# Row factors in place of the padding, the neighbourhood bias from 157 numbers per partition, and the first normalised block scaled on VectorE

## The chip, the cores and the metric

The kernel runs on one core of a Trainium2 chip. A core has five engines that run their own instruction queues side by side and meet at semaphores: TensorE (PE, matrix products), VectorE (DVE) and ScalarE (ACT, both element by element), GpSimd (POOL, a general engine) and SyncE (SP, which here issues every transfer between memory and the core). Data lie in an on-chip memory of 128 partitions; a tile is a rectangle of partitions by bytes in each. The metric is the device time of one execution in microseconds (us), less is better.

## What is computed

Two different transformer blocks follow one another on 256 tokens of width 1024, two layers each, in float32. Shortened to what matters here:

```
x = layer_norm(x, ln_in_g, ln_in_b)
for l in range(2):                                   # first block
    proj = x @ w_in[l]                               # 6816 columns: three attentions and gates
    na   = neighbourhood_attention(...)              # scores + rpb bias, masked, softmax
    df   = diff_attention(...)
    mla  = latent_attention(...)
    merged = sum(gate_i * (branch_i @ w_branch[l, i]))
    x = layer_norm(ALPHA * x + merged @ w_out[l])
    gu = x @ w_ffn_in[l]
    x = layer_norm(ALPHA * x + (silu(gu[:2816]) * gu[2816:]) @ w_ffn_out[l])
for i in range(2):                                   # second block
    ... norm, projection w_in_2, attention and spatial gating, w_o_2
    ... norm, w_up_2, depthwise convolution, silu * up, w_down_2

# neighbourhood attention, head h: tokens on a 4 x 64 grid
sc = q @ k.T * 64 ** -0.5
sc = sc + rpb[h, row offset, column offset]          # rpb: (8 heads, 15, 31)
sc = where(column inside the query's own 16, sc, -inf)
```

## The kernel before

Every large product is made of float32r matmuls on numbers split in two: a high part `hi` and a rest `lo`. `mm3` adds hi x hi, hi x lo and lo x hi into one accumulator, so lines L254, L255 and L256 are its three matmuls. The activations of a stage lie in the tiles `xh` and `xl` (8 chunks of 128 rows by 256 tokens). The weights come by SyncE in blocks called `raw` (up to 1 MB, three buffers, L183). ACT casts a piece of a block into its high part (`high`, L188), DVE subtracts it for the low part (`low`, L192), both into slots of the pool `s4` (30 slots of 4608 bytes). When a block's last piece is split, `low` issues the next block's transfer. A matmul has a stationary operand (128 columns that are loaded first) and a moving operand (256 or 512 columns). `gemm_a` holds the activations stationary and moves 512 columns of weights (a row of the profile names it `ps<-s,xh`: out, moving, stationary). `gemm_b` holds the weights stationary and moves the 256 tokens (`ps<-xh,s`); there the splits are stored 64 bytes (high) and 192 bytes (low) into their slot (`OFF_HI`, `OFF_LO`). Where the activations are themselves in `s4`, as for a branch's output or the FFN's inner values, the rows read `ps<-s,s`.

The order is the program's own: a list of steps that `emit` walks through, in which `turns` mixes attention heads with products (`fill`), and `pump` splits the next pieces ahead of use. Nothing is reordered when it runs: each engine takes its queue in order.

Neighbourhood attention (in each of the first block's two layers) runs eight heads. `na_bias(h)` loads the bias of a head for the 128 query partitions: a partition is a query's (reversed) column in one of two grid rows, and takes 64 numbers of each of four grid rows from `rpb`, at an address that grows by one number from partition to partition. The mask (0 or -1e30) is then added on GpSimd (L852). `na_scores(h)` first calls `na_bias(h + 3)`, then makes the scores, adds the bias on DVE (L863) and takes the softmax; ACT scales the result (L829) and TensorE transposes it (L406). The tiles for these come from the pool `s2`, 12 buffers of 2048 bytes.

At the start `head` normalises the tokens by halves (`t`): statistics on DVE (L493), transposes on TensorE (L530), scale and shift by `ln_in` on ACT (`in_high`, L537, four activations), a cast into `xh` (L538), and the rest into `xl` on DVE (`in_low`, L542).

The tiles that live for the whole program are allocated in `constants`, one behind the other, each rounded up to 32 bytes; behind them lie the pools `raw`, `s4`, `s2`, `gb`, `st`.

Of the kernel before, what the change touches and what calls it, by code (L numbers as in the profile page):

```python
# [10 lines left out]
F32 = mybir.dt.float32  # L11
F32R = mybir.dt.float32r
AF = mybir.ActivationFunctionType
ALU = mybir.AluOpType
# [3 lines left out]
P = 128  # L18
# [8 lines left out]
RMS_EPS = 1e-6  # L27
MASKED = -1e30

X_PAD = 8
WARM = (0, 0)

RAW_BUFS = 3
S4_BUFS = 30
# [79 lines left out]
class Net:  # L116
# [295 lines left out]
    def constants(self):  # L412
        nc, a, cp = self.nc, self.a, self.cp
        self.x_tok = cp.tile([P, 2, D], F32, name="x_tok")
        self.xh = cp.tile([P, KT, 256], F32R, name="xh")
        self.xl = cp.tile([P, KT, 256], F32R, name="xl")
        self.fixed = cp.tile([P, a["c_fixed"].shape[1]], F32, name="fixed")
        cp.tile([P, X_PAD], F32, name="pad")
        self.neghalf = cp.tile([P, 20], F32, name="neghalf")
        nc.vector.memset(self.neghalf, -0.5)  # L420
        self.ones = cp.tile([P, 1], F32, name="ones")
        nc.vector.memset(self.ones, 1.0)
        self.col = cp.tile([P, a["c_vectors"].shape[1]], F32, name="col")
        self.row = cp.tile([P, 2], F32, name="row")
        self.neglam = cp.tile([P, DEPTH], F32, name="neglam")
        for c in range(2):
            cs = slice(c * 512, c * 512 + 512)
            nc.sync.dma_start(self.x_tok[:, 0, cs], a["x"][0, :P, cs])
        nc.sync.dma_start(self.fixed[:, :P + 2 * KT], a["c_fixed"][:, :P + 2 * KT])
        self.ident = self.fixed[:, :P]  # L430
        self.ln_in = [self.fixed[:, P + i * KT:P + (i + 1) * KT] for i in range(2)]
        o = P + 2 * KT

        def table(n):
            nonlocal o
            o += 4 * n
            return self.fixed[:, o - 4 * n:o].rearrange("p (a t n) -> p a t n", a=2, t=2)

        self.rope_df, self.rope_mla, self.rope_gqa = table(16), table(32), table(64)
        self.mask = self.fixed[:, o:o + 64]  # L440
# [91 lines left out]
    def in_high(self, t, c):  # L532
        nc, y, ps = self.nc, self.s2([P, 4, P]), self.in_ps[t, c]
        self.in_y[t, c] = y
        for k in range(4):
            g, b = (v[:, 4 * c + k:4 * c + k + 1] for v in self.ln_in)
            nc.scalar.activation(y[:, k, :], ps[:, k * P:k * P + P], AF.Identity, scale=g, bias=b)  # L537
        nc.scalar.copy(self.xh[:, 4 * c:4 * c + 4, t * P:t * P + P], y)  # L538

    def in_low(self, t, c):  # L540
        ks, ts = slice(4 * c, 4 * c + 4), slice(t * P, t * P + P)
        self.nc.vector.tensor_tensor(self.xl[:, ks, ts], self.in_y[t, c], self.xh[:, ks, ts], op=ALU.subtract)  # L542

    def warm(self, n):

        for _ in range(n):
            self.nc.tensor.matmul(self.warm_ps[:, :P], self.warm_in, self.warm_in, start=True, stop=True)

    def head(self, dfq, dfk):


        self.in_scale, self.in_ps, self.in_y = {}, {}, {}

        def first():
            if WARM[0]:
                self.warm_in, self.warm_ps = self.s2([P, P]), self.psum()
                self.nc.gpsimd.memset(self.warm_in, 1.0)
            self.warm(WARM[0])
            self.in_stats(0)
            self.in_norm(0)  # L560
            self.in_trans(0)
            self.warm(WARM[1])
            self.high(0)
            self.in_high(0, 0)
            self.in_stats(1)
            self.low_next()
            self.in_low(0, 0)
            self.high(1)
            self.low_next()
            self.in_high(0, 1)  # L570
            self.in_norm(1)
            self.in_low(0, 1)

        def second():
            self.in_trans(1)
            self.high(2)
            self.low_next()
            self.high(3)

        def third():  # L580
            self.in_high(1, 0)
            self.low_next()
            self.in_low(1, 0)
            self.in_high(1, 1)

        self.add(first, dfq[:2], second, dfq[2], third, dfq[3], lambda: self.in_low(1, 1), self.lookahead(AHEAD_EDGE), dfq[4:], dfk)

    def in_rows(self, t):
# [62 lines left out]
    def attention_1(self, l):  # L651
        nc, a = self.nc, self.a
        w = a["w_in"][l]
# [187 lines left out]
            S["mlap", h] = (p, sm)  # L841

        def na_bias(h):
            b = self.s2([P, 2, 256])
            rpb = a["na_rpb"]
            for q in range(2):
                for r in range(2):
                    o = rpb.offset + (l * 8 + h) * 465 + (7 - 2 * q - r) * 31 - 48
                    nc.sync.dma_start(b[r * 64:r * 64 + 64, q, :].rearrange("p (r c) -> p r c", r=4),
                                        bass.AP(tensor=rpb.tensor, offset=o, ap=[[1, 64], [31, 4], [1, 64]]))  # L850
            v = b.rearrange("p q (r c) -> p (q r) c", r=4)
            nc.gpsimd.tensor_tensor(v, v, self.mask.unsqueeze(1).broadcast_to([P, 8, 64]), op=ALU.add)  # L852
            S["bias", h] = b

        def na_scores(h):
            if h + 3 < 8:
                na_bias(h + 3)
            ps, p = self.psum("at"), self.s2([P, 512])
            nmx, sm = self.st(2), self.st(2)
            r = slice(64 * (h % 2), 64 * (h % 2) + 64)  # L860
            for q in range(2):
                nc.tensor.matmul(ps[:, q * 256:q * 256 + 256], S["naqT"][r, h // 2, q * P:q * P + P], S["nakT"][r, h // 2, :], start=True, stop=True)
            nc.vector.tensor_tensor(p, ps, S["bias", h].rearrange("p q k -> p (q k)"), op=ALU.add)  # L863
            self.row_exp(p, p, nmx, sm)
            S["nap", h] = (p, sm)
# [88 lines left out]

        fill = gate("df", 1, 0) + late + gate("df", 1, 1) + branch("df", 1, 0, 0) + branch("df", 1, 1, 0) + gate("mla", 2, 0)
        fill.append(Step(lambda: [na_bias(h) for h in range(3)]))
        self.add(turns([(value("mla", "mv"), 3), (trans("mla"), 2), (normalize("mla"), 1), (mla_scores, 0), 1], 8, fill))

# [467 lines left out]
```

## Time and profile before

| | |
|---|---|
| median of 3 runs | 1506.68 us (1506.45 to 1506.7) |
| profiled execution | 1504.22 us, of which the span from first to last instruction is 1502.4 us |
| busy in the span | PE 98%, DVE 66%, ACT 55%, POOL 6% |
| transfers | 260.44 MB, mean 173 GB/s |

The profile is one execution, taken by the hardware. TensorE's matmuls overlap each other in it and their ends are modelled, so how fast it streams is read from the starts of successive matmuls, and how much it loses from its waits. Waits of an engine that is not late for anyone cost nothing.

### The profile page before, as it was taken

To read this page: it belongs to the slowest core of one execution; us is meant where nothing else is said; L and a number is where in the kernel's file an instruction comes from. 1 tells how busy PE (TensorE), PEld (TensorE's weight loads), DVE (VectorE), ACT (ScalarE), POOL (GpSimd) and SP (SyncE) were. 2 spreads that over 40 slices of the span, in tenths; PEclk is the share of its full clock that TensorE was granted. 3 is DMA by queue.
4 is the path that set the end of the run, shared out by engine and by line. 5 is a ranking of instruction groups with operands and counts; after the bars stand their busy time and mean duration, and the time that the engine had idled before them with its cause. 6 is when DMAs were issued, how large, how long until landed. Compare 5 with 4: busy or idle time off the path is not lost.

```text
span 1502.4 us, 23794 instructions
## 1 busy us (share of the span) xinstructions
PE 1478.0 (98%) x9616; PEld 1314.7 (88%) x9616; DVE 990.2 (66%) x1434; ACT 822.8 (55%) x1387; POOL 90.3 (6%) x116
## 2 busy tenths in 40 slices
PE   7999999999999999999999999999999999999998
PEld 5889988899988889998889998777999887789987
DVE  5786655855556676556775555876788758669881
ACT  6664566444442565656444443675767536568660
POOL 0000020000000000011000000310000012000000
PEclk9999999999999999999999999999999999999999
DMA  7744565576563654466665564553565735255660
GB/s 242 249 138 153 177 115 177 168 225 196 193 229 98 203 162 141 147 146 169 201 224 182 178 215 140 183 180 113 164 199 194 254 124 193 74 168 169 199 222 28
DMA packets 179021, 260.44 MB, mean 173 GB/s; under 512 B 23648, under 2 KB 122208, under 8 KB 178912
## 3 DMA queue, kind: packets, MB, share of 16 engines
q1 hardware_dynamic: 178912, 258.93, 54.4%
q8 instruction: 75, 1.23, 0.3%
q14 instruction: 34, 0.28, 0.1%
HBM read 257.86 MB, written 1.05 MB: 172 GB/s over the span
## 4 chain that ended last, share of the span: by engine, by line
PE 48%; DVE 3%; ACT 0%; issue 0%; POOL 0%; DVEq 0%; POOLq 0%; ACTq 0%
PE ps L254 15%; PE ps L256 15%; PE ps L255 15%; DVE s L192 1%; PE ps L1142 1%; PE ps L390 1%; PE ps L406 1%; PE ps L642 0%; DVE x_tok L505 0%; DVE st L493 0%; PE ps L1191 0%; DVE s L492 0%; PE ps L1298 0%; PE ps L1181 0%; DVE s L913 0%
## 5 line engine op out<-in xcount | busy, mean ns | idle before, releaser
L192 DVE TENSOR_TENSOR s<-raw,s 128x1024 fp32r<-128x1024 f32 (+2 forms) x468 | 553.9, 1211 | 175.4 <-ACT s L188 126.6
L188 ACT CAST s<-raw 128x1024 fp32r<-128x1024 f32 (+2 forms) x468 | 466.3, 1039 | 117.1 <-PE ps L255 26.4
L254 PE MATMUL ps<-xh,s 128*128 128x256 f32 x1664 | 475.6, 286 | 1.9 <-DVE s L738 1.4
L255 PE MATMUL ps<-xl,s 128*128 128x256 f32 x1664 | 468.0, 281 | 0.0
L256 PE MATMUL ps<-xh,s 128*128 128x256 f32 x1664 | 466.4, 280 | 0.0
L254 PEld LDWEIGHTS ps<-xh,s 128*128 128x128 f32 x1664 | 313.2, 188 | 10.1 <-issue 6.5
L255 PEld LDWEIGHTS ps<-xl,s 128*128 128x128 f32 x1664 | 317.7, 191 | 0.5
L256 PEld LDWEIGHTS ps<-xh,s 128*128 128x128 f32 x1664 | 314.0, 189 | 0.0
L254 PE MATMUL ps<-s,s 128*128 128x512 f32 (+1 forms) x712 | 259.4, 364 | 0.0
L255 PE MATMUL ps<-s,s 128*128 128x512 f32 (+1 forms) x712 | 254.6, 358 | 0.0
L256 PE MATMUL ps<-s,s 128*128 128x512 f32 (+1 forms) x712 | 254.4, 357 | 0.0
L254 PE MATMUL ps<-s,xh 128*128 128x512 f32 (+3 forms) x448 | 171.8, 383 | 3.6 <-ACT xh L538 3.2
L256 PE MATMUL ps<-s,xl 128*128 128x512 f32 (+3 forms) x448 | 169.6, 379 | 1.0 <-DVE xl L351 1.0
L255 PE MATMUL ps<-s,xh 128*128 128x512 f32 (+3 forms) x448 | 169.2, 378 | 0.0
L254 PEld LDWEIGHTS ps<-s,s 128*128 128x128 f32 x712 | 133.7, 188 | 29.2 <-issue 10.0
L256 PEld LDWEIGHTS ps<-s,s 128*128 128x128 f32 x712 | 133.7, 188 | 20.5
L255 PEld LDWEIGHTS ps<-s,s 128*128 128x128 f32 x712 | 133.8, 188 | 18.4
L254 PEld LDWEIGHTS ps<-s,xh 128*128 128x128 f32 x448 | 84.6, 189 | 20.0 <-ACT xh L538 3.6
L256 PEld LDWEIGHTS ps<-s,xl 128*128 128x128 f32 x448 | 84.5, 189 | 19.5 <-DVE xl L351 3.0
L255 PEld LDWEIGHTS ps<-s,xh 128*128 128x128 f32 x448 | 84.7, 189 | 15.8 <-DVE s L192 0.5
L361 POOL TENSOR_SCALAR st<-st 128x2 f32<-128x2 f32 (+2 forms) x46 | 24.2, 525 | 963.6 <-DVE st L500 456.9
L400 ACT ACTIVATE s<-ps,st 128x256 f32<-128x256 f32 x96 | 44.6, 472 | 50.2 <-DVE st L397 49.7
(177 smaller groups left out, 1253.6 us busy)
## 6 DMA issues: line engine op xcount, KB each, us to landing
raw<-in_w_in SPq DMA_DIRECT2D x61, 1024.0 KB, 5.2
raw<-in_w_ffn_in SPq DMA_DIRECT2D x88, 512.0 KB, 5.1
raw<-in_w_up SPq DMA_DIRECT2D x88, 512.0 KB, 5.0
raw<-in_w_ffn_out SPq DMA_DIRECT2D x22, 1024.0 KB, 5.0
raw<-in_w_down SPq DMA_DIRECT2D x22, 1024.0 KB, 5.0
raw<-in_w_branch SPq DMA_DIRECT2D x12, 1024.0 KB, 5.3
raw<-in_w_out SPq DMA_DIRECT2D x8, 1024.0 KB, 5.0
raw<-in_w_o SPq DMA_DIRECT2D x8, 1024.0 KB, 5.0
```

The costliest lines, as they stand in the source:

```text
L188: nc.scalar.copy(u.hi, u.raw.tile[:, u.off:u.off + u.nk, :])
L192: nc.vector.tensor_tensor(u.lo, u.raw.tile[:, u.off:u.off + u.nk, :], u.hi, op=ALU.subtract)
L254: mm(out, lh, rh, start=first, stop=False, skip_group_check=skip)
L255: mm(out, lh, rl, start=False, stop=False, skip_group_check=skip)
L256: mm(out, ll, rh, start=False, stop=last, skip_group_check=skip)
L361: self.nc.gpsimd.tensor_scalar(v, src, scale, eps, op0=ALU.mult, op1=ALU.add)
L390: self.nc.tensor.matmul(o[r, :256], vs[:, r] if vs.shape[1] == P else vs, pts[i][:, k * 256:k * 256 + 256], start=k == 0, stop=k == 1)
L400: nc.scalar.activation(p[:, qs], src[:, qs], AF.Exp, bias=nmx[:, q:q + 1], accum_out=sm[:, q:q + 1])
L406: self.nc.tensor.transpose(ps[:, k * 256 + q * P:k * 256 + q * P + P], p[:, q * 256 + k * P:q * 256 + k * P + P], self.ident)
L1142: nc.tensor.matmul(ps[:, q * 256:q * 256 + 256], S["qT"][r, h % 4, q * P:q * P + P], S["kT"][r, :], start=True, stop=True)
```

## The change

Three places change. `constants` no longer allocates 8 unused numbers (`pad`, 32 bytes) behind `fixed`; `row`, the two factors per partition of the second block's norms, moves there from behind `col`. `in_high` does the first of its four blocks (`t == c == 0`) by two operations on DVE, the scale and the shift of a vector per chunk, read with a stride of zero along the tokens; the other three stay on ACT. `na_bias` loads 157 consecutive numbers per partition (3 x 31 + 64) into a tile `w` of its own, and the mask's addition reads its four overlapping rows of 64 from there, one addition for each `q`. The functions that made idle products at the start (`warm`, count 0) go.

```diff
-X_PAD = 8
-WARM = (0, 0)
...
         self.fixed = cp.tile([P, a["c_fixed"].shape[1]], F32, name="fixed")
-        cp.tile([P, X_PAD], F32, name="pad")
+
+        self.row = cp.tile([P, 2], F32, name="row")
         self.neghalf = cp.tile([P, 20], F32, name="neghalf")
...
         self.col = cp.tile([P, a["c_vectors"].shape[1]], F32, name="col")
-        self.row = cp.tile([P, 2], F32, name="row")
...
     def in_high(self, t, c):
         nc, y, ps = self.nc, self.s2([P, 4, P]), self.in_ps[t, c]
         self.in_y[t, c] = y
-        for k in range(4):
-            g, b = (v[:, 4 * c + k:4 * c + k + 1] for v in self.ln_in)
-            nc.scalar.activation(y[:, k, :], ps[:, k * P:k * P + P], AF.Identity, scale=g, bias=b)
+        if t == c == 0:
+            g, b = (v[:, :4].unsqueeze(2).broadcast_to([P, 4, P]) for v in self.ln_in)
+            nc.vector.tensor_tensor(y, ps.rearrange("p (k n) -> p k n", k=4), g, op=ALU.mult)
+            nc.vector.tensor_tensor(y, y, b, op=ALU.add)
+        else:
+            for k in range(4):
+                g, b = (v[:, 4 * c + k:4 * c + k + 1] for v in self.ln_in)
+                nc.scalar.activation(y[:, k, :], ps[:, k * P:k * P + P], AF.Identity, scale=g, bias=b)
...
         def na_bias(h):
-            b = self.s2([P, 2, 256])
+
+            b, w = self.s2([P, 2, 256]), self.s2([P, 2, 157])
             rpb = a["na_rpb"]
             for q in range(2):
                 for r in range(2):
                     o = rpb.offset + (l * 8 + h) * 465 + (7 - 2 * q - r) * 31 - 48
-                    nc.sync.dma_start(b[r * 64:r * 64 + 64, q, :].rearrange("p (r c) -> p r c", r=4),
-                                        bass.AP(tensor=rpb.tensor, offset=o, ap=[[1, 64], [31, 4], [1, 64]]))
-            v = b.rearrange("p q (r c) -> p (q r) c", r=4)
-            nc.gpsimd.tensor_tensor(v, v, self.mask.unsqueeze(1).broadcast_to([P, 8, 64]), op=ALU.add)
+                    nc.sync.dma_start(w[r * 64:r * 64 + 64, q, :], bass.AP(tensor=rpb.tensor, offset=o, ap=[[1, 64], [1, 157]]))
+            for q in range(2):
+                v, s = b[:, q, :].rearrange("p (r c) -> p r c", r=4), w[:, q, :]
+                s = bass.AP(tensor=s.tensor, offset=s.offset, ap=[s.ap[0], [31, 4], [1, 64]])
+                nc.gpsimd.tensor_tensor(v, s, self.mask.unsqueeze(1).broadcast_to([P, 4, 64]), op=ALU.add)
             S["bias", h] = b
```

The allocation has an effect that the diff doesn't show: 32 bytes fewer stand ahead of the pools. Where the tiles begin in each partition of the built programs, in bytes, with the remainder by 64 (all slots of a pool have the same remainder; the two offsets of stationary weights, 64 and 192, keep it):

| tile or pool | before | after |
|---|---|---|
| x_tok | 2176 (0) | 2176 (0) |
| xh | 10368 (0) | 10368 (0) |
| xl | 18560 (0) | 18560 (0) |
| fixed | 26752 (0) | 26752 (0) |
| row | 31328 (32) | 29376 (0) |
| neghalf, ones, col | 29408, 29504, 29536 | the same |
| neglam | 31360 (0) | 31328 (32) |
| raw, first buffer | 31392 (32) | 31360 (0) |
| s4, first slot | 55968 (32) | 55936 (0) |
| s2, first buffer | 194208 (32) | 194176 (0) |
| g, b | 218784, 222880 (32) | 218752, 222848 (0) |

On every engine the instructions stand in the order of before but at two places. The first is the start of the program. On DVE, before, the statistics of the second half (`L493`, second time) stand right behind the normalising of the first (`L523`):

```order
L493 BN_STATS st_104<-x_tok 128x6 x2
L516 BN_AGGR st_107<-st_104 128x2
L523 TENSOR_SCALAR x_tok<-x_tok,st_107,st_110 128x512 x2
L493 BN_STATS st_133<-x_tok 128x6 x2
L516 BN_AGGR st_136<-st_133 128x2
L192 TENSOR_TENSOR s_16_142<-raw_96,s_10_125 128x1024
L542 TENSOR_TENSOR xl<-s_11_127,xh 128x4x128
```

and now (line numbers have shifted: L489 is the statistics, L519 the normalising, L188 the low part of a weight, L543 `in_low`):

```order
L489 BN_STATS st_103<-x_tok 128x6 x2
L512 BN_AGGR st_106<-st_103 128x2
L519 TENSOR_SCALAR x_tok<-x_tok,st_106,st_109 128x512 x2
L533 TENSOR_TENSOR s_11_126<-ps_114,fixed 128x512
L534 TENSOR_TENSOR s_11_126<-s_11_126,fixed 128x512
L489 BN_STATS st_130<-x_tok 128x6 x2
L512 BN_AGGR st_133<-st_130 128x2
L188 TENSOR_TENSOR s_16_139<-raw_95,s_10_124 128x1024
L543 TENSOR_TENSOR xl<-s_11_126,xh 128x4x128
```

Two operations have come in between L519 and the second statistics; on ACT the four activations of L537 between the first cast of a weight and the cast into `xh` are gone.

The second is the neighbourhood bias. On GpSimd in the first layer, before, the four additions that stand first (one for a head, both `q` at once, in place):

```order
L362 TENSOR_TENSOR st_1265<-st_1264,neghalf 128x2
L852 TENSOR_TENSOR s_395_2072<-s_395_2072,fixed 128x512
L852 TENSOR_TENSOR s_396_2078<-s_396_2078,fixed 128x512
L852 TENSOR_TENSOR s_397_2084<-s_397_2084,fixed 128x512
L852 TENSOR_TENSOR s_398_2090<-s_398_2090,fixed 128x512
```

and now:

```order
L358 TENSOR_TENSOR st_1262<-st_1261,neghalf 128x2
L845 TENSOR_TENSOR s_395_2069<-s_396_2070,fixed 128x256 x2
L845 TENSOR_TENSOR s_397_2077<-s_398_2078,fixed 128x256 x2
L845 TENSOR_TENSOR s_399_2085<-s_400_2086,fixed 128x256 x2
L845 TENSOR_TENSOR s_401_2093<-s_402_2094,fixed 128x256 x2
```

Each addition has become two of half the size, and reads another `s2` tile (`w`) than it writes. On SyncE, where the same four transfers per head stand at the same places between the weight blocks, before:

```order
L183 DMA raw_2030<-in_w_in 128x4x512
L849 DMA s_395_2072<-in_na_rpb 64x4x64 x4
L849 DMA s_396_2078<-in_na_rpb 64x4x64 x4
L849 DMA s_397_2084<-in_na_rpb 64x4x64 x4
L849 DMA s_398_2090<-in_na_rpb 64x4x64 x4
L183 DMA raw_2136<-in_w_in 128x4x512
```

and now, with one run of 157 numbers for four of 64 in each of 64 partitions:

```order
L179 DMA raw_2027<-in_w_in 128x4x512
L841 DMA s_396_2070<-in_na_rpb 64x157 x4
L841 DMA s_398_2078<-in_na_rpb 64x157 x4
L841 DMA s_400_2086<-in_na_rpb 64x157 x4
L841 DMA s_402_2094<-in_na_rpb 64x157 x4
L179 DMA raw_2141<-in_w_in 128x4x512
```

Nothing has moved past another transfer there.

## Rows read from the trace of the kernel before

**Rows 1.** The page, busy us, share of the span and instructions of each engine.

```profile
PE 1478.0 (98%) x9616; PEld 1314.7 (88%) x9616; DVE 990.2 (66%) x1434; ACT 822.8 (55%) x1387; POOL 90.3 (6%) x116
```

**Rows 2.** Groups by line and shape, PE: count | busy us, mean ns | idle before.

```profile
L254 PE MATMUL ps<-xh,s 128*128 128x256 f32 x1664 | 475.6, 286 | 1.9 <-DVE s L738 1.4 <-ACT s L738 0.5
L254 PE MATMUL ps<-s,s 128*128 128x512 f32 x508 | 201.6, 397 | 0.0
L254 PE MATMUL ps<-s,xh 128*128 128x512 f32 x352 | 142.1, 404 | 3.6 <-ACT xh L538 3.2 <-ACT xh L350 0.4
L254 PE MATMUL ps<-s,s 128*128 128x256 f32 x204 | 57.8, 284 | 0.0
L642 PE MATMUL ps<-fixed,s 128*128 128x128 f32 x64 | 8.3, 272 | 0.0
L642 PE MATMUL ps<-fixed,x_tok 128*128 128x128 f32 x48 | 6.6, 274 | 0.7 <-DVE x_tok L505 0.7
```

**Rows 3.** Timeline of PE, start us, us, line: first and last of four stretches.

```profile
25.07 0.39 PE L255 MATMUL ps<-s,xh 128*128 128x512 f32 x1
...
36.97 0.39 PE L255 MATMUL ps<-s,xh 128*128 128x512 f32 x1
...
258.19 0.28 PE L255 MATMUL ps<-s,s 128*128 128x256 f32 x1
...
268.85 0.28 PE L256 MATMUL ps<-s,s 128*128 128x256 f32 x1
...
345.03 0.28 PE L254 MATMUL ps<-xh,s 128*128 128x256 f32 x1
...
404.98 0.28 PE L256 MATMUL ps<-xh,s 128*128 128x256 f32 x1
...
440.18 0.39 PE L255 MATMUL ps<-s,s 128*128 128x512 f32 x1
...
471.91 0.39 PE L254 MATMUL ps<-s,s 128*128 128x512 f32 x1
```

**Rows 4.** Windows: us, busy of PE, PEld, DVE, ACT, POOL; PEclk, DMA share, GB/s.

```profile
1057.00:1160.00 103.00, 103.00 (x877) 103.00 (x876) 84.64 (x135) 75.43 (x115) 0.00 (x0) 1.00 0.55 179
190.00:205.00 15.00, 15.00 (x110) 13.39 (x109) 6.22 (x9) 8.40 (x19) 4.62 (x3) 1.00 0.60 62
235.66:239.07 3.41, 3.41 (x14) 2.76 (x13) 0.54 (x2) 2.60 (x6) 0.62 (x1) 0.50 0.97 366
699.87:703.28 3.41, 3.41 (x19) 3.41 (x18) 0.00 (x0) 1.49 (x4) 0.98 (x1) 0.50 0.65 248
```

**Rows 5.** Groups by line and shape, DVE: count | busy us, mean ns | idle before.

```profile
L351 DVE TENSOR_TENSOR s<-s,s 128x512 fp32r<-128x512 f32 x40 | 27.4, 685 | 3.1 <-ACT s L350 3.1
L351 DVE TENSOR_TENSOR xl<-ps,xh 128x512 fp32r<-128x512 f32 x28 | 17.9, 683 | 11.0 <-ACT xh L350 11.0
```

**Rows 6.** Transfers by source: count, KB each, median us from issue to landing.

```profile
raw<-in_w_branch SPq DMA_DIRECT2D x12, 1024.0 KB, 5.3
```

**Rows 7.** Waits of PE: who waited for whom, us in all, times, longest.

```profile
PE ps L406 <- ACT s L829: 3.6, 2, 2.0
```

**Rows 8.** Timelines of SP and ACT around the first layer's neighbourhood heads.

```profile
222.65 0.55 SPq L183 DMA_DIRECT2D raw<-in_w_branch  x1
223.30 4.04 SPq L849 DMA_DIRECT2D s<-in_na_rpb  x4
...
231.75 1.05 ACT L188 CAST s<-raw 128x1024 fp32r<-128x1024 f32 x1 [3.96 <-DMA raw<-in_w_branch]
```

**Rows 9.** Timeline of the start, PE, ACT and DVE.

```profile
6.74 1.97 PE L530 MATMUL ps<-fixed,x_tok 128*128 128x128 f32 x8 [6.74 <-DVE x_tok L523]
...
9.70 1.50 ACT L537 ACTIVATE s<-ps,fixed 128x128 f32<-128x128 f32 x4
10.03 1.29 DVE L493 BATCH_NORM_STATS2 st<-x_tok 128x6 f32<-128x512 f32 x2 [2.89 <-DMA x_tok<-in_x]
...
11.48 1.18 DVE L192 TENSOR_TENSOR s<-raw,s 128x1024 fp32r<-128x1024 f32 x1
```

More of the change, by code (lines that the diff above doesn't have):

```diff
@@ L542, in in_low @@
         self.nc.vector.tensor_tensor(self.xl[:, ks, ts], self.in_y[t, c], self.xh[:, ks, ts], op=ALU.subtract)
-    def warm(self, n):
-        for _ in range(n):
-            self.nc.tensor.matmul(self.warm_ps[:, :P], self.warm_in, self.warm_in, start=True, stop=True)
     def head(self, dfq, dfk):
@@ L554, in first @@
         def first():
[L555 to L558, printed above, removed]
             self.in_stats(0)
@@ L561, in first @@
             self.in_trans(0)
-            self.warm(WARM[1])
             self.high(0)
```

## The prediction

> **What bounds the kernel now.** I read the page's engine line first. TensorE (PE) is busy 1478.0 of 1502.4 us, VectorE (DVE) 66%, ScalarE (ACT) 55%, GpSimd (POOL) 6% [rows 1]. So time falls only where TensorE streams faster or loses one of its few waits. The reader should note which groups make up its work: 1664 matmuls of 256 columns on each of the three lines of `mm3`, moving `xh`/`xl` over a weight in `s`, and 352 of 512 columns on each, moving a weight over `xh`/`xl` [rows 2]. Next I read starts of matmuls in four undisturbed stretches, first and last row of each, and divided by the steps between. 256 columns, `x` moving over `s`: 345.03 to 404.98, 510 matmuls, 59.95/509 = 117.8 ns a step. 256 columns, `s` over `s`: 258.19 to 268.85, 95 matmuls, 10.66/94 = 113.4 ns. 512 columns, `s` over `x`: 25.07 to 36.97, 52 matmuls, 11.90/51 = 233.3 ns. 512 columns, `s` over `s`: 440.18 to 471.91, 141 matmuls, 31.73/140 = 226.6 ns [rows 3]. Same shapes, same loops, no waits, yet a matmul with an `x` tile in it takes 4.4 ns (256) or 6.7 ns (512) more. Last I read the waits of TensorE, ACT's and SyncE's timeline around the longest, and windows for the clock and the transfers; they come with their term below.
>
> **The row factors in the padding's place.** The code's work is unchanged; addresses are not. In the table of addresses ahead, `xh`, `xl` and `fixed` begin at a multiple of 64 bytes before and after. The pools `raw`, `s4`, `s2`, `gb` began 32 bytes past a multiple of 64, and now begin on one. In the trace of before every `x`-with-`s` pair is therefore mixed (remainders 0 and 32), and every `s`-with-`s` pair equal (32 and 32). The slots of `s4` differ in every higher address bit, and steps within a class do not, so I take the low bits for the cause: a mixed pair is slow, an equal pair fast. After the change all pairs are equal (0 and 0). Bounds for a mixed pair: it saves nothing (the pair of two zeros is as slow, or the remainder is not the cause), or the whole difference. I take the whole difference, as the `s`-with-`s` rows are the nearest: gate, FFN and branch stages share `gemm_b`, its shapes and its accumulators. Against it stand the f32 transposes, which take 272 ns from `s` and 274 ns from `x_tok`, both over `fixed` [rows 2]: there the remainder does nothing.
>
> Sum: 3 x 1664 x 4.4 ns = 22.0 us; 3 x 352 x 6.7 ns = 7.1 us; the 288 matmuls of 384, 288 and 256 columns with stationary `x` have no equal partner, and at 4.4 to 6.7 ns give 1.3 to 1.9 us, say 1.5. Together 30.6 us. Can the others follow? The fullest stretch is the second block's FFN, DVE 84.64 of 103.00 us, ACT 75.43, transfers 0.55 of their engines [rows 4]; 4% less time leaves DVE at 86%. I keep 95%: **29 us**; bounds 0 and 30.6. DVE gains nothing by it: `hilo`'s subtraction of 128x512 means 685 ns on `s` alone and 683 ns into `xl` from `xh` [rows 5].
>
> The Trainium skill, "SBUF — State Buffer", section "Who interferes with whom", speaks against this term: it gives TensorE two independent SBUF read ports, one for the moving operand and one for the weight load, and names no address that matters. By it this term would be 0 and the time 1500.7. The trace's 113.4 against 117.8 ns does not agree with it as it stands, unless something other than addresses parts the two classes.
>
> **The neighbourhood bias.** Before, each head loads 4 x 64 x 4 = 1024 pieces of 64 numbers (256 B), 16 heads 16,384. Now it loads 256 pieces of 157 numbers (628 B), 4,096 in all; bytes fall from 16,384 x 256 = 4.19 MB to 4,096 x 628 = 2.57 MB. From 190 to 205 us, where such pieces dominate, the transfer engines are busy 0.60 and move 62 GB/s; in the FFN 0.55 moves 179 [rows 4]. Neither row prices a piece of 628 B. By pieces the load costs 1/4 of before, by bytes 0.61; both are less, and I take 0.4.
>
> What it is worth is read where TensorE waits: on ACT's L829 twice, 3.6 us in all [rows 7], once in each layer. Follow the first back. SyncE issues a raw block of `w_branch` at 222.65, then four bias loads that occupy it 4.04 us, about 1 us each; ACT's next cast idles 3.96 us for that block and begins at 231.75 [rows 8]. That is 9.1 us after the issue, where such blocks land in 5.3 at the median [rows 6]. The cast and L829 queued behind it are late, and TensorE with them. From 235.66 and from 699.87 the granted clock is 0.50, the lower level, for 3.41 us each, after those waits [rows 4]; at half speed that costs 1.7 us each. The stall is worth 3.6 + 3.4 = 7.0 us. If the block lands in 5.3 us (228.0), the wait is gone with 3.8 us to spare. I take **6 us**, bounds 0 and 7.0.
>
> The added costs: POOL runs two additions of 256 for one of 512, at 6% busy; each head takes a second of the 12 `s2` buffers. A bias load that waits for its buffer holds the raw blocks behind it on SyncE, and an addition that waits holds the next heads' additions, and so L863 on DVE. The order shows the same places for all SyncE rows. The loads run three heads ahead, and today's addition already waits on the transfer, so I cost this at 0; uncovered, it is the 3.6 us wait again.
>
> **The first block on VectorE.** ACT loses four activations of 1.50 us; DVE gains two operations of 128x512, about 0.69 us each by the 683 to 685 ns of [rows 5]. They fall into the 2.89 us that DVE idles before L493 at 10.03, which waits for `x` [rows 9]; the eight transposes end too early to push past it (their first four are done when half the 1.97 us from 6.74 are over) [rows 9]. `xh` is ready 1.5 us earlier, and TensorE's first product with it. The second needs L192, at 11.48 to 12.66 on DVE [rows 9], behind the same L493: the chain is as late as before. I take **0**; bounds: 0.7 us gained if TensorE's clock rises up to 1.5 us sooner (half speed there), 0.5 lost if the two operations are twice as long and push L493.
>
> **The sum.** The profiled execution took 1504.22 us, span 1502.4 and 1.82 around it; the median of the three runs is 1506.68, 2.46 more. 1504.2 - 29 - 6 - 0 = 1469.2; against the median **1471.7 us**, 2.3% less.
>
> **Rivals.**
> - *Addresses do nothing.* What parts the classes would be the tiles themselves. For it: the transposes. Against it: within a stretch the weights come from many slots and the chunks of `xh` change, and the steps stay level. Only the bias gains: 1506.7 - 6 = 1500.7. (The Trainium skill's "SBUF — State Buffer", "Who interferes with whom", sides with this one.)
> - *Slower: two zeros are a bad pair.* The trace has no f32r pair with both remainders 0. If a zero on either side is what costs, the `x` pairs stay slow and the 2136 `s`-with-`s` ones become so: 3 x 508 x 6.7 + 3 x 204 x 4.4 = 12.9 us [rows 2]. With the bias's 6: 1506.7 + 12.9 - 6 = 1513.6. It decides once two zeros cost over 35/8472 = 4.1 ns more than two 32s, as all 8472 `mm3` matmuls pay it and 29 + 6 us stand against it.
> - *The bias wait stays*, since a later block is late instead or a buffer wait replaces it: 1506.7 - 29 = 1477.7. This is in the first forecast's range.
>
> **How the numbers follow.** Equal pairs fast: 0.75 (with the stall gone or not), own range 1465 to 1484: low 1506.7 - 30.6 - 7.0 - 0.7 = 1468.4 and 3 us for the reading of the steps, high 1506.7 - 23 = 1484 with three quarters of 30.6 and the whole stall left. Addresses do nothing: 0.13, 1500.7. Two zeros bad: 0.10, 1513.6. A mixture that cancels: 0.02. A measurement tells 0.2% (3 us) from no change. Faster: 0.75 and most of the 0.13, 0.86; within 0.2%: 0.03; slower 0.11. The likeliest case holds under eight in ten, so the range reaches to the second: 1465 to 1502.
>
> **What would show it.** Right: in the FFN, 510 matmuls in 57.8 us and not 59.95; 233 ns falls to 227 in the 512-column stretches with stationary `x`; `s`-with-`s` steps stay. TensorE's wait on L829 is gone and the clock stays at the higher level through 240 and 703 us. The first product starts near 10.4 us, the third still near 13.3. Wrong: steps of 117.8 unchanged (addresses do nothing), or 113.4 grown to 117 or more (two zeros bad), or a DVE wait that fills the FFN.

## The result and the profile after

The changed kernel takes 1470.5 us, the median of 3 runs (1469.54 to 1470.88), against 1506.68 before: a ratio of 0.9759, 95% interval 0.9737 to 0.9781. The profiled execution is the one of 1470.5 us, with a span of 1468.7. One profile further below (the run with weights 96 bytes into their slots) was taken while the granted clock stood at 0.85; of that kernel only the time is used.

The page of the kernel after, engine line and packets, answers to [rows 1]:

```profile
PE 1447.5 (99%) x9616; PEld 1290.7 (88%) x9616; DVE 990.0 (67%) x1436; ACT 820.9 (56%) x1383; POOL 93.9 (6%) x132
...
DMA packets 166733, 258.82 MB, mean 176 GB/s; under 512 B 7264, under 2 KB 109920, under 8 KB 166624
```

TensorE lost 30.5 us of busy time with the same 9616 matmuls; the busy times of the other engines hardly changed (POOL's grew by 3.6 us). TensorE's timeline after (start us, duration us, engine, line), first and last matmul of three stretches, answers to [rows 3]:

```profile
25.18 0.40 PE L250 MATMUL ps<-s,xh 128*128 128x512 f32 x1
...
36.99 0.39 PE L251 MATMUL ps<-s,xh 128*128 128x512 f32 x1
...
335.03 0.28 PE L250 MATMUL ps<-xh,s 128*128 128x256 f32 x1
...
394.98 0.28 PE L251 MATMUL ps<-xl,s 128*128 128x256 f32 x1
...
430.14 0.39 PE L251 MATMUL ps<-s,s 128*128 128x512 f32 x1
...
461.87 0.39 PE L250 MATMUL ps<-s,s 128*128 128x512 f32 x1
```

They hold 53, 530 and 141 matmuls: 11.81/52 = 227 ns, 59.95/529 = 113.3 ns and 31.73/140 = 226.6 ns a step. The first two were 233.3 and 117.8 and have fallen to what the pairs without an `x` tile had before; the third has not moved.

The waits of TensorE after (us in all, times, longest), the first five:

```profile
PE ps L526 <- DVE x_tok L519: 6.7, 1, 6.7
PE ps L250 <- ACT xh L539: 1.7, 1, 1.7
PE ps L251 <- DVE s L188: 1.5, 1, 1.5
PE ps L250 <- DVE s L729: 1.4, 2, 0.7
PE ps L252 <- DVE xl L347: 1.2, 1, 1.2
```

The wait of the neighbourhood heads' transposes on ACT [rows 7] is gone (L402 and L820 would be its lines now). Windows after answer to [rows 4]:

```profile
190.00:205.00 15.00, 15.00 (x114) 13.37 (x113) 8.66 (x13) 10.41 (x25) 5.81 (x8) 1.00 0.89 187
235.66:239.07 3.41, 3.41 (x30) 2.76 (x29) 1.00 (x3) 3.27 (x8) 0.00 (x0) 1.00 0.45 183
350.00:390.00 40.00, 40.00 (x356) 40.00 (x355) 22.07 (x23) 19.57 (x24) 0.00 (x0) 1.00 0.55 179
440.00:465.00 25.00, 25.00 (x114) 20.70 (x113) 12.08 (x16) 4.12 (x5) 1.22 (x2) 1.00 0.38 129
1030.00:1130.00 100.00, 100.00 (x875) 99.65 (x875) 85.13 (x136) 75.87 (x115) 0.00 (x0) 1.00 0.55 181
```

At 235.66 the granted clock is 1.00; nowhere between the start (it rises at 16.3 us) and the last 2 us is there a stretch at the lower level. In 1030 to 1130, the second block's FFN, DVE is at 85% and ACT at 76%, and neither holds TensorE up. The row of 350 to 390 also shows a short way to read a step, used below. A window also counts the matmuls that only reach into it, so its length plus one matmul's duration is divided by their number: (40 + 0.28)/356 = 113.1 ns.

SP's and ACT's timelines after, around the first layer's heads, answer to [rows 8]:

```profile
207.75 0.37 SPq L179 DMA_DIRECT2D raw<-in_w_branch  x1
208.22 2.38 SPq L841 DMA_DIRECT2D s<-in_na_rpb  x4
216.64 0.37 SPq L179 DMA_DIRECT2D raw<-in_w_branch  x1
...
220.04 1.99 ACT L184 CAST s<-raw 128x1024 fp32r<-128x1024 f32 x2
...
228.38 1.03 ACT L184 CAST s<-raw 128x1024 fp32r<-128x1024 f32 x1
```

A head's four loads occupy SyncE 2.38 us, and ACT's casts carry no idle time for a block. By the list of transfers a bias load now lands 4.0 us after its issue at the median:

```profile
raw<-in_w_branch SPq DMA_DIRECT2D x12, 1024.0 KB, 5.1
...
s<-in_na_rpb SPq DMA_DIRECT2D x64, 39.2 KB, 4.0
```

Before it took 8.4 us:

```profile
s<-in_na_rpb SPq DMA_DIRECT2D x64, 64.0 KB, 8.4
```

The start after, PE and DVE, answers to [rows 9]:

```profile
10.43 0.80 PE L250 MATMUL ps<-s,xh 128*128 128x512 f32 x1 [1.73 <-ACT xh L539]
12.77 0.79 PE L251 MATMUL ps<-s,xh 128*128 128x512 f32 x1 [1.54 <-DVE s L188]
13.37 0.80 PE L252 MATMUL ps<-s,xl 128*128 128x512 f32 x1
...
7.89 0.69 DVE L533 TENSOR_TENSOR s<-ps,fixed 128x512 f32<-128x512 f32 x1 [0.75 <-PE ps L526]
8.62 0.69 DVE L534 TENSOR_TENSOR s<-s,fixed 128x512 f32<-128x512 f32 x1
10.09 1.29 DVE L489 BATCH_NORM_STATS2 st<-x_tok 128x6 f32<-128x512 f32 x2 [0.78 <-DMA x_tok<-in_x]
```

The first product starts 1.5 us earlier, the second waits for `low` as foretold, and the third starts at 13.37.

So far all is as predicted. But the reason given for the steps was a guess from two classes, and the sizes had not been tried apart. The experiments do both.

### The profile page after: what moved, and what is told of

Its sections match the earlier page's. It is cut to its first block, busy times and chain, and to the rows that moved or that the text cites. A ratio compares the mean times of both kernels' runs of the same rounds, so it can differ in the third digit from the quotient of the medians.

```text
span 1468.7 us, 23788 instructions
## 1 busy us (share of the span) xinstructions
PE 1447.5 (99%) x9616; PEld 1290.7 (88%) x9616; DVE 990.0 (67%) x1436; ACT 820.9 (56%) x1383; POOL 93.9 (6%) x132
## 4 chain that ended last, share of the span: by engine, by line
PE 87%; DVE 7%; ACT 3%; DMA 2%; issue 1%; POOL 0%; SPq 0%; DVEq 0%; ACTq 0%; POOLq 0%
PE ps L250 26%; PE ps L252 25%; PE ps L251 25%; DVE s L188 3%; PE ps L402 2%; PE ps L386 2%; DMA raw<-in_w_in 1%; PE ps L1135 1%; PE ps L855 1%; PE ps L830 1%; PE ps L633 1%; ACT s L396 1%; DMA x_tok<-in_x 1%; ACT s L184 0%; PE ps L740 0%
## 5 line engine op out<-in xcount | busy, mean ns | idle before, releaser
L188 DVE TENSOR_TENSOR s<-raw,s 128x1024 fp32r<-128x1024 f32 (+2 forms) x468 | 552.8, 1209 | 166.1 <-ACT s L184 119.0
L250 PE MATMUL ps<-xh,s 128*128 128x256 f32 x1664 | 466.1, 280 | 1.9 <-DVE s L729 1.4
L252 PE MATMUL ps<-xh,s 128*128 128x256 f32 x1664 | 460.0, 276 | 0.0
L251 PE MATMUL ps<-xl,s 128*128 128x256 f32 x1664 | 459.8, 276 | 0.0
L251 PEld LDWEIGHTS ps<-xl,s 128*128 128x128 f32 x1664 | 312.6, 188 | 0.5
L250 PE MATMUL ps<-s,xh 128*128 128x512 f32 (+3 forms) x448 | 169.9, 379 | 2.1 <-ACT xh L539 1.7
L251 PE MATMUL ps<-s,xh 128*128 128x512 f32 (+3 forms) x448 | 167.1, 373 | 1.5 <-DVE s L188 1.5
L251 PEld LDWEIGHTS ps<-s,s 128*128 128x128 f32 x712 | 133.8, 188 | 18.4
```

What stands on the lines that cost most here:

```text
L188: nc.vector.tensor_tensor(u.lo, u.raw.tile[:, u.off:u.off + u.nk, :], u.hi, op=ALU.subtract)
L250: mm(out, lh, rh, start=first, stop=False, skip_group_check=skip)
L251: mm(out, lh, rl, start=False, stop=False, skip_group_check=skip)
L252: mm(out, ll, rh, start=False, stop=last, skip_group_check=skip)
```

## The experiments

Twelve kernels were measured in four groups, each beside the kernel before, which took 1504.5 to 1505.0 us there. The 1470.5 us stand beside the 1506.68, so times across the two are comparable to about 2 us. "Distance" below is the stationary operand's start minus the moving one's, taken by 128 bytes (its remainder). For the pairs in question it was 96 in the kernel before (`x` over `s` in 256 columns: 64 + 32; `s` over `x` in 512: 0 - 32), and is 64 and 0 after; the pairs without an `x` tile have 64 and 0 in both.

### Each part by itself

**The address alone.** Before, with only this edit:

```diff
-        cp.tile([P, X_PAD], F32, name="pad")
```

> The kernel before without the 32 bytes of padding, and no other edit: the pools begin at a multiple of 64 bytes, the bias is loaded as before, the first block stays on ACT. If the address remainder sets the step of the split matmuls, 117.8 ns falls to 113.4 and 233.3 to 226.6 and the time is 1506.7 - 29 = 1478 us, with TensorE's wait behind the neighbourhood heads still there. If the addresses do nothing and the gain came with the bias, it stays at 1506.7.

1484.68 us, ratio 0.9862 (0.9846 to 0.9878). Its windows in an FFN stretch and at the heads:

```profile
350.00:390.00 40.00, 40.00 (x355) 40.00 (x354) 23.28 (x24) 17.97 (x22) 0.00 (x0) 1.00 0.62 200
...
233.44:240.27 6.83, 6.78 (x25) 5.44 (x25) 2.73 (x5) 3.49 (x9) 1.28 (x1) 0.50 0.75 261
```

its waits of TensorE:

```profile
PE ps L406 <- ACT s L828: 6.1, 5, 2.4
```

and its ACT timeline:

```profile
230.76 1.04 ACT L188 CAST s<-raw 128x1024 fp32r<-128x1024 f32 x1 [4.79 <-DMA raw<-in_w_branch]
```

The steps are those of after (40.28/355 = 113.5 ns). The stall did not stay as it was: TensorE's waits grew from 3.6 us, two times, to 6.1 us, five times. The time at granted clock 0.50 is 6.83 us as before, but in one stretch at the first layer's heads, where before has two of 3.41, one in each layer. The block is issued earlier too (220.70 us against 222.65), but ACT's cast now begins 10.1 us after the issue, where before it was 9.1.

**The bias alone.** Before, with the new `na_bias` and nothing else:

```diff
-            b = self.s2([P, 2, 256])
+            b, w = self.s2([P, 2, 256]), self.s2([P, 2, 157])
...
-                    nc.sync.dma_start(b[r * 64:r * 64 + 64, q, :].rearrange("p (r c) -> p r c", r=4),
...
+                    nc.sync.dma_start(w[r * 64:r * 64 + 64, q, :], bass.AP(tensor=rpb.tensor, offset=o, ap=[[1, 64], [1, 157]]))
...
```

> The kernel before with the new loading of the neighbourhood bias alone. My term: TensorE's two waits on the scaled probabilities (3.6 us) and the two stretches at the lower clock (3.4 us) go, 1506.7 - 6 = 1500.7 us, at most 1499.7. If the stall only moves to the next late block: 1506.7.

1495.5 us, ratio 0.9935 (0.9922 to 0.9948): 9.5 us, not 6. The wait and the half-clock stretches are gone. SyncE's timeline shows where the time comes from. In the kernel before, the eight bias loads that stand ahead of the late block of `w_branch` (issued at 222.65, [rows 8]):

```profile
209.53 13.02 SPq L849 DMA_DIRECT2D s<-in_na_rpb  x8
```

and here:

```profile
201.52 5.82 SPq L850 DMA_DIRECT2D s<-in_na_rpb  x8
...
210.73 0.37 SPq L183 DMA_DIRECT2D raw<-in_w_branch  x1
```

TensorE is equally far in both kernels (the table of matmuls below, 1400), so the block is issued 11.9 us earlier; and it lands 5.3 us after its issue, where before it took 9.1.

**The first block alone.** Before, with the new `in_high`:

```diff
...
+        if t == c == 0:
+            g, b = (v[:, :4].unsqueeze(2).broadcast_to([P, 4, P]) for v in self.ln_in)
+            nc.vector.tensor_tensor(y, ps.rearrange("p (k n) -> p k n", k=4), g, op=ALU.mult)
+            nc.vector.tensor_tensor(y, y, b, op=ALU.add)
...
```

> The kernel before with the first normalised block scaled on VectorE alone. My term: 0, as the second product waits for VectorE in either case; first product near 10.4 us, third near 13.3. Bounds: 0.7 us less if the clock rises sooner, 0.5 more. If the start is bound by ACT's chain: 1.4 us less.

1504.76 us, ratio 0.9999 (0.9987 to 1.0012): nothing that this measurement, good to some 2 us, can see.

**Address and bias together**, the first block left on ACT:

```diff
-        cp.tile([P, X_PAD], F32, name="pad")
...
-            b = self.s2([P, 2, 256])
+            b, w = self.s2([P, 2, 256]), self.s2([P, 2, 157])
...
```

> Before without the 32 unused bytes and with the new bias load, first block left on ACT. If the two edits make the whole gain and only fail to add up when each is tried alone (the stall at the neighbourhood heads grows once TensorE streams faster, and the bias load removes it whole): 1470.5 us, no wait of TensorE on the normalise of the softmax, no half-clock stretch after the start, steps 113 and 227 ns. If the first block on VectorE is worth something once the rest is gone: 1471 to 1473. If the sum of the two single runs were right (20.3 and 9.5 off): 1475.

1471.65 us, ratio 0.9775 (0.9758 to 0.9792). 1504.88 - 1471.65 = 33.2, where the two alone give 20.3 + 9.5 = 29.8: by the medians the bias load is worth 13.0 us once the steps are short, and the address 23.9 us once the stall is gone. The intervals of the three ratios overlap here (26 to 35 us for the sum, 31 to 36 for both), so the excess rests on the traces that follow.

Where the parts fall can be read from single matmuls: the n-th matmul (counted from 0) is the same one in all these kernels, so its start says how far each has come (start in us after the span's start; from the traces):

```
matmul   before   bias alone   address alone   both    changed kernel
1400      221.1      221.1         219.9       218.6       217.8
1600      250.5      246.5         250.7       243.4       242.6
4400      670.4      666.3         663.6       655.8       654.9
4800      725.6      717.5         718.6       706.4       705.5
9600     1494.6     1486.5        1474.3      1462.1      1461.2
```

The bias load wins 4.0 us between matmuls 1400 and 1600 (the first layer's heads) and 4.0 us between 4400 and 4800 (the second layer's), and nothing elsewhere. "Both" then shrinks steadily against "bias alone". With the old loads the two stretches take 84.6 us together at the long steps and 85.8 us at the short ones; with the new loads 76.6 and 75.4. So at the heads shorter steps win nothing while the old loads hold the blocks up: in these traces the bias load is worth 8.0 us before the address edit and 10.4 us behind it.

The last two columns differ by 0.9 us, all of it from the first 100 us. The clock rises at 15.8 to 17.3 us in nine traces with the first block on VectorE (that of the weights 96 bytes in left out), and at 16.8 to 18.4 in the four without; their matmul 100 starts at 34.4 to 35.7 us and at 35.1 to 35.7. Half a microsecond of gain is possible; the times can't tell it from none.

### Is it the remainder by 64?

**Pools 32 bytes further on.** The changed kernel with 32 unused bytes put back, so that the pools begin 32 past a multiple of 64:

```diff
         self.row = cp.tile([P, 2], F32, name="row")
+        cp.tile([P, 8], F32, name="pad")
```

> The changed kernel with 32 unused bytes per partition ahead of the pools again, so that all pools begin 32 bytes past a multiple of 64. Address theory: steps back at 117.8 and 233 ns, 1470.5 + 29 = 1500 us, while the wait behind the neighbourhood heads stays gone. If the addresses do nothing: 1470.5.

1495.2 us, ratio 0.9934 (0.9919 to 0.9948). Windows:

```profile
350.00:390.00 40.00, 40.00 (x342) 40.00 (x341) 20.06 (x21) 14.76 (x19) 0.00 (x0) 1.00 0.64 207
```

342 matmuls, 117.8 ns a step, as before the change. Against the changed kernel, matmul by matmul, the 4934 steps of `x` over `s` in 256 columns took 4.2 ns more on average (20.8 us), the 1028 of `s` over `x` in 512 columns 4.4 ns (4.5 us), all others together 0.7 us less: 24.6 us, where the times differ by 24.7. (Steps to a following product of another kind are among the others.)

**Pools 64 bytes further on.** The remainder by 64 stays 0 everywhere:

```diff
         self.row = cp.tile([P, 2], F32, name="row")
+        cp.tile([P, 16], F32, name="pad")
```

> The changed kernel with 64 unused bytes ahead of the pools: every address behind moves, but the remainder by 64 stays 0. If the remainder by 64 is what counts: 1470.5 us, steps 113.4 and 226.6 ns. If the exact distance between the x tiles and the pools counts (a remainder by 128 or more): steps change, and the time with them, by up to the 29 us of the address term.

1495.44 us, ratio 0.9936 (0.9921 to 0.9951). Windows:

```profile
350.00:390.00 40.00, 40.00 (x340) 40.00 (x340) 20.32 (x21) 14.99 (x19) 0.00 (x0) 1.00 0.63 209
```

118.5 ns a step with all remainders equal. **The reason of the prediction, equal remainders by 64, is refuted.** The distance of the operands by 128 became 0 for 256 columns, and 64 for `s` over `x` in 512, whose steps are 230 ns, neither 227 nor 234.

### Is it the pair, or where the tiles lie?

**Moving weights 32 bytes into their slot.** The changed kernel, in `gemm_a` alone:

```diff
-            u.hi = self.s4([P, u.nk, u.n], F32R, OFF_HI if u.stationary else 0)
+            u.hi = self.s4([P, u.nk, u.n], F32R, OFF_HI if u.stationary else 8)
...
-            u.lo = self.s4([P, u.nk, u.n], F32R, OFF_LO if u.stationary else 0)
+            u.lo = self.s4([P, u.nk, u.n], F32R, OFF_LO if u.stationary else 8)
```

> The changed kernel with the moving weights of gemm_a stored 32 bytes into their slots; the stationary weights of gemm_b stay. Now stationary s tiles over moving s tiles are mixed pairs too (0 and 32). Address theory: every 512-column step becomes 233 ns, also those between s tiles that were never slow: 3 x (352 + 508) x 6.7 ns = 17.3 us, and 2 to 3 us for the narrower ones, about 1490 us; gemm_b stays at 113.4. If the x tiles themselves were the slow ones, the steps between s tiles stay at 226.6 and the time at 1470.5.

1481.71 us, ratio 0.9845 (0.983 to 0.986). Windows, an FFN stretch of 256 columns and one of 512 without an `x` tile:

```profile
350.00:390.00 40.00, 40.00 (x356) 40.00 (x355) 21.31 (x22) 19.58 (x24) 0.00 (x0) 1.00 0.55 181
440.00:465.00 25.00, 25.00 (x109) 20.11 (x108) 11.16 (x13) 5.15 (x5) 1.23 (x2) 1.00 0.44 147
```

25.39/109 = 233 ns, where it was 226.6: pairs of two `s` tiles become slow too. So it is not the `x` tiles. Some 20 us were expected and 11.2 measured: matmul by matmul, the 512-column steps grew by 5.8 ns (`s` over `s`, 8.5 us) and 4.3 ns (`s` over `x`, 4.4 us) on average, and the narrower products added nothing.

**Stationary weights at the start of their slot.**

```diff
-OFF_HI, OFF_LO = 16, 48
+OFF_HI, OFF_LO = 0, 0
```

> The changed kernel with the stationary weights of gemm_b stored at the start of their slots, not 64 and 192 bytes into them. The remainder by 64 is 0 as before. If that alone counts: 1470.5 us. If a finer relation counts (the same remainder by 128), the 256-column steps grow by some 6 ns, which the few 256-column steps of gemm_a in the changed kernel hint at (119 ns, in stages with other shapes between): 5568 x 6 ns = 33 us, about 1503 us.

1503.86 us, ratio 0.999 (0.9979 to 1.0001): the whole gain is lost, the bias load's too. Windows:

```profile
350.00:390.00 40.00, 40.00 (x335) 40.00 (x335) 21.68 (x23) 16.38 (x21) 0.00 (x0) 1.00 0.60 198
```

40.28/335 = 120.2 ns: the longest step of 256 columns in all these runs, though the same distance 0 is the best in 512. With the pools 64 bytes further on these pairs also have both starts on a multiple of 128, and take 118.5 ns.

**Moving weights 64 bytes into their slot** (the edit as with 8 numbers, now 16):

```diff
-            u.hi = self.s4([P, u.nk, u.n], F32R, OFF_HI if u.stationary else 0)
+            u.hi = self.s4([P, u.nk, u.n], F32R, OFF_HI if u.stationary else 16)
...
```

> The changed kernel with the moving weights of gemm_a stored 64 bytes into their slots. By the remainder by 64 nothing changes: 1470.5 us. If gemm_a gains from a distance of 64 bytes to its stationary operand as gemm_b may, its narrower steps fall by some 6 ns (288 and 612 of them: up to 5 us), and the 512-column steps of 226.6 perhaps too (2580 of them).

1474.42 us, ratio 0.9794 (0.9776 to 0.9812). Windows:

```profile
440.00:465.00 25.00, 25.00 (x111) 20.54 (x110) 11.84 (x14) 5.15 (x5) 1.23 (x2) 1.00 0.43 146
```

25.39/111 = 229 ns. The distance that is good in 256 columns costs 2 ns in 512.

**Everything 32 bytes off but the stationary weights.** The kernel with 32 unused bytes, and its offsets smaller by 32 bytes:

```diff
+        cp.tile([P, 8], F32, name="pad")
...
-OFF_HI, OFF_LO = 16, 48
+OFF_HI, OFF_LO = 8, 40
```

> The changed kernel with its pools 32 bytes further on (as in the run with 8 unused numbers, 1495.2 us), but the stationary weights of gemm_b stored 32 and 160 bytes into their slots, so that they begin at the very addresses of the changed kernel while every other tile of the pools stays 32 bytes off. If only the distance of the two operands' starts counts: the 256-column steps of x over s fall from 118 to 113 ns, the 512-column steps of s over x stay at 234, time about 1495.2 - 22 = 1473 plus 0 to 3 for the 612 products of 256 columns whose two operands are now 32 bytes apart, 1473 to 1476. If it is the place of the pools (transfers, ACT and DVE writing there): 118 ns stays and 1495.

1476.03 us, ratio 0.9805 (0.9788 to 0.9822). Windows:

```profile
350.00:390.00 40.00, 40.00 (x355) 40.00 (x354) 20.26 (x21) 19.04 (x24) 0.00 (x0) 1.00 0.57 183
```

Against the kernel of 1495.2 us only the place of the stationary weights within their slots differs, and 117.8 ns become 113.5. `raw`, `s2`, `g` and `b` still lie where they did before the change. It is the place of the operands, and not what transfers, ACT or DVE do with the pools.

That the stationary operand's own start is not enough, the pairs of two `s` tiles in the same run show. Their stationary weights begin 64 past a multiple of 128, as those under `x` do, but their moving operand begins at 32 and not at 0. A stretch of them here, and the same one in the changed kernel, where it begins at 0:

```profile
251.60:262.60 11.00, 11.00 (x95) 11.00 (x95) 7.53 (x10) 6.88 (x10) 0.00 (x0) 1.00 0.58 182
```

```profile
250.10:260.60 10.50, 10.50 (x95) 10.50 (x94) 7.05 (x9) 6.37 (x10) 0.00 (x0) 1.00 0.60 190
```

11.28/95 = 118.7 ns against 10.78/95 = 113.5. The same remainder of the stationary operand gives both steps; what decides is the place of the two operands to each other.

**Stationary weights 32 and 160 bytes into their slots**, in the changed kernel:

```diff
-OFF_HI, OFF_LO = 16, 48
+OFF_HI, OFF_LO = 8, 40
```

> The changed kernel with the stationary weights of gemm_b 32 and 160 bytes into their slots, so that they begin 32 bytes past a multiple of 128 while the moving activations begin on one. Distances 0 and 96 were slow for 256 columns (118 to 120 ns) and 64 fast (113). If 64 alone is fast: 118 ns at 32 as well, 5604 products x 4.4 ns = 24.7 us, 1495. If 32 and 64 are both fast: 113 ns and 1470.5.

1495.18 us, ratio 0.9933 (0.992 to 0.9947). Windows:

```profile
350.00:390.00 40.00, 40.00 (x340) 40.00 (x339) 20.51 (x22) 15.21 (x19) 0.00 (x0) 1.00 0.64 210
```

118.5 ns. **Moving weights 96 bytes into their slots** (the edit with 24 numbers):

```diff
-            u.hi = self.s4([P, u.nk, u.n], F32R, OFF_HI if u.stationary else 0)
+            u.hi = self.s4([P, u.nk, u.n], F32R, OFF_HI if u.stationary else 24)
...
```

> The changed kernel with gemm_a's moving weights 96 bytes into their slots, so that the activations which it holds stationary begin 32 bytes behind them (mod 128). Of the four distances in steps of 32 bytes this is the one not yet seen with 512 columns: 0 gave 227 ns, 64 gave 229 to 230, 96 gave 234. If only a distance of 0 is good and 32 is as 96: 234 ns, and as in the run with the weights 32 bytes into their slots about 1482. If the step grows from distance 0 on as 0, 32, 64: 228 to 229, 1472 to 1474. If 32 is the best place for 512 columns, steps under 227 ns and a time under 1470, a kernel faster than the changed one.

1482.03 us, ratio 0.9842 (0.9819 to 0.9864): as the run with 32 bytes. The steps of all runs by distance, medians in ns (from starts of successive matmuls in the traces and addresses of the programs):

| distance by 128 | 256 columns | 512 columns |
|---|---|---|
| 0 | 118 (pools +64), 120 (offsets 0) | 227 |
| 32 | 118 | not read; the time is that of 96 |
| 64 | 113 | 229 to 230 |
| 96 | 118 | 234 |

The changed kernel has the best of each column, and none of the runs beat it. That 0 gives 118 in one run and 120 in another says that the distance by 128 is not the whole rule either. Nor are the three matmuls of `mm3` alike within a cell: at 96 in 256 columns their median steps are 119, 119 and 116 ns, at 64 in 512 columns 226, 229 and 232 (moving weights at 64 bytes, `s` over `s`).

## Why the prediction was right, and where its reasons failed

**The time** was forecast at 1471.7 and is 1470.5, and the mechanism that carried it, TensorE's steps getting shorter by the operands' addresses, is shown by the two kernels that differ only in where the stationary weights begin in their slots (1495.2 and 1476.03 us). That it came within 1.2 us is in part luck, as the sizes below show.

**The step that failed: "a mixed pair is slow, an equal pair fast".** Remainders by 64 that are equal gave 118.5 ns with the pools 64 bytes further on, and 120.2 with the offsets at 0. The number still came out, since the change gives the `x` pairs exactly the distances of the pairs without an `x` tile from which the steps were read: 64 and 0. Two classes that differ in one low bit could not tell the remainder from the distance. The transposes, which stood against the term, are a case of their own: their median step from `s` is 109 ns whether the stationary operand begins 32 bytes behind the moving one (before), 0 (after) or 64 (pools 64 bytes further on).

**The size of the address term.** 30.6 us were counted and 29 taken; 24 were measured (23.9 and 24.7). The 256-column part gave 20.8 for 22.0. The 512-column part gave 4.5 to 4.9 for 7.1, since its mean step fell by 4.4 to 4.8 ns and not by 6.7, and steps to another kind of product not at all. The 1.5 us for the products without an equal partner came to 0.1: 384 and 288 columns won 1.1 to 1.2 ns a step, and 256 columns of `s` over `x` went from 117 to 120 ns, as their distance became 0.

**The size of the bias term.** 6 us were taken with an upper bound of 7.0; it is 9.5 alone and 13.0 after the address. The chain from the late block through ACT's cast to L829 holds: the wait, the block's lateness and the stretches at half clock went together. Three things were missed. First, the forecast kept the block's issue at 222.65 us and let it only land sooner; with the new loads alone it is issued 11.9 us earlier, as the eight bias loads ahead of it keep SyncE for 5.82 us and not 13.02. (The 3.8 us "to spare" are not spare either: TensorE's wait there is 2.0 of them.) Second, the rows of the wait and the clock made 7.0 us, but the starts of matmuls show 8.1 lost at the two places; where the other 1.1 lies is open. The median difference of 9.5 is more than the trace's 8.1 because the stall is not the same in every execution: before takes 1503.3 us on average where its mean granted clock is 0.999 (14 executions) and 1507.7 where it is 0.995 (4), while the kernel with the new loads takes 1494.9 to 1495.9 in all six, at 1.000. Third, I added the terms as if they were independent, but under the old loads the heads take as long with short steps as with long ones. The two errors, 5 us too much and 3 to 7 too little, nearly cancel.

**The added costs at nothing** (two additions on POOL, a second `s2` buffer) hold: SyncE's bias loads wait 2.6 us in all after the change, 13.1 before, and DVE's bias additions wait 4.2 us for POOL, two times:

```profile
POOL s L845: 4.2, 2
```

Before it was twelve times:

```profile
POOL s L852: 35.2, 12
```

**The first block at 0** fits its own run, which is good to some 2 us and can't see the 0.7 and 0.5 us of its bounds; the starts in the traces leave room for half a microsecond of gain.

**The rivals.** "Addresses do nothing" is refuted. The Trainium skill's "SBUF — State Buffer", section "Who interferes with whom", gives TensorE independent read ports for the moving operand and the weight load and names no address. The traces do not agree that these two reads are indifferent to each other: the stationary operand moved by 32 bytes against the moving one gives 113 or 118 ns. "Two zeros are a bad pair" did not happen in the change, but the run with offsets at 0 shows that it would have with other offsets: 120 ns in 256 columns. "The bias wait stays" did not happen with the bias edit and did without it.

**Open:** what in the reading of the operands makes the distance count, and why 256 and 512 columns want different ones.

## What to carry to other kernels

Where matmuls follow one another with a new weight each time, compare the steps of one shape between operand pairs; if they differ by some per cent, move one operand by 32 or 64 bytes inside its slot and measure, for each width apart. An allocation that looks like padding may hold such a distance, and any edit that adds 32 bytes in front of it may undo it. When an edit makes the bounding engine faster, re-price every wait on a transfer that does not get faster with it: the terms need not add. And a transfer of many small pieces delays what stands behind it in the queue twice, at its issue and at its landing: look at both times.

## What the runs showed of the hardware that was not expected

- The step of successive f32r matmuls depends on where the stationary operand starts against the moving one: 113 ns at a distance of 64 bytes by 128, and 118 to 120 at 0, 32 and 96, in 256 columns; 227 at 0, 229 to 230 at 64 and 234 at 96 in 512.
- The best distance of one width is a bad one of the other: offsets at 0 cost 33 us in this kernel, and moving weights at 64 bytes 4 us.
- A transfer of a quarter as many pieces landed in 4.0 us instead of 8.4, with 61% of the bytes, and SyncE was occupied 2.38 us by the four of one head instead of 4.04, and 5.82 us by eight instead of 13.02, waits included. The 1 MB block behind them landed 5.3 us after its issue instead of 9.1.
